# Later sums of the decays, later transposes of the context's convolved tiles

## The chip, the cores and the metric

The kernel runs on one core of a Trainium2 chip. Times are device microseconds (us) of that core. TensorE multiplies matrices, VectorE (DVE in the profile), ScalarE (ACT) and GpSimd (POOL) work on tiles in SBUF and PSUM, SyncE (SP) issues most of the DMAs. PE is TensorE, PEld its weight loads. Lower is better.

## The reference

One layer of a hybrid diffusion backbone on 512 latent tokens and a prefix of 256 context tokens, model width 1024, float32:

```
hc  = modulate(rmsnorm(ctx), csh1, csc1)          # 256 context tokens
pc  = hc @ w_in[:, :XBCDT_COLS]                   # x, B, C and dt columns
xbc_c = silu(dwconv_centred(pc[..., :CONV_CH], conv_w, conv_b))   # 5 taps along the tokens
init_states = final SSD state of the context, forward and backward
hx  = modulate(rmsnorm(x), sh1, sc1)              # 512 latent tokens
p   = hx @ w_in                                   # x, B, C, dt, gate z, pooling columns
y_x = SSD scan of both directions over 4 chunks of 128 tokens, started from init_states
x   = x + g1 * (concat(rmsnorm(y_x * silu(z)), pooling(p)) @ w_out)
x   = x + g2 * moe(modulate(rmsnorm(x), sh2, sc2))     # top 4 of 32 experts, d_ff 1024
out = rmsnorm(x)
```

The scan has 24 heads in four groups of six. The decays are `log_a = -exp(a_log) * softplus(dt)`; the scan uses their running sums within a chunk and the exponentials of these. The final state of the context is a sum over its tokens of B times (x times a weight `wdec` made from these sums).

## The kernel before, in words

The work goes in stages: modulation (to about 40 us), norms and transposes (to about 60), the context stage (to about 275), the scan of the four head groups (to about 560), the output projection and the router, and the experts (from about 600 to the end).

Products in float32 are done in three passes: `split_weights` makes a rounded part `hi` of a weight tile (L228, ScalarE) and the remainder `lo` (L231, VectorE, or every second one GpSimd for the scan's projections), and three matmuls follow: L353, L354 and L355 in `token_major`, L336, L337 and L338 in the scan's `project`. A 512-wide matmul is one of these. Weight tiles come by SyncE's DMAs into a ring `raw` of 6; `hi` and `lo` have rings of 3.

The context stage is a loop over the four groups g (L557). In each turn:

- `z_block` (turns 0, 1 and 3): the gate columns of the latent tokens, four accumulators, then tanh (L369, ScalarE) and L370 (VectorE).
- `ctx_conv(g)`: the context's projected columns (tile `ctxp`, tokens by channels) are convolved in two halves of two 128-channel blocks. A half is: four transposes to channels by tokens into a PSUM bank (L447), a copy into `xp` (L452, ScalarE), one first tap for each block (L456) and four further ones (L459) on VectorE into `ac`, tanh (L462, ScalarE), the product (L389, VectorE), four transposes back (L467) and a copy into `xc` (L468, ScalarE). `xp` and `ac` have two buffers each, `xc` two.
- `ctx_proj(g + 1)`: the next group's projection, two accumulators, copied to `ctxp`.
- `mod_row(g)`: one 1024-wide row of the modulation of the second sub-layer. Eight 512 KB blocks of w_mod come by SyncE (L417) into `mraw`, a ring of three that the bias takes part in. Even blocks go over ScalarE (L419) and a sum on GpSimd (L421), odd ones are summed on VectorE (L423, L425); L426 (GpSimd) adds both, and L432 sums over the partitions on TensorE, followed by L434 (VectorE).
- `ctx_state(g)`: `chunk_state` scales `xc` by `wdec` (L407, GpSimd) and multiplies (L409, TensorE); L477 (ScalarE) keeps the state.

Ahead of the loop stand the first `ctx_proj(0)`, the columns of dt with their softplus, and the sums of the decays (L521 to L552), which make `wdec`, `ecs` and `etot`.

The written order is not what runs. The framework's scheduler takes the instructions of the whole program, estimates times for them, and picks for each engine the order in which they stand in its queue; written order is one input of it. So projections of the scan's first group (L336 to L338, with taps L374 and L378) already run among the context's work. What each engine then does in a row is fixed when the kernel is built; at run time an engine takes its queue in that order and waits at an instruction whose inputs are not there.

Of the kernel before, what the change touches and what calls it, by code (L numbers as in the profile page):

```python
# [5 lines left out]
F32 = mybir.dt.float32  # L6
# [4 lines left out]
AF = mybir.ActivationFunctionType  # L11
ALU = mybir.AluOpType
# [4 lines left out]
P = 128  # L17
# [80 lines left out]
def mixer_and_moe(tc, a):  # L98
    nc = tc.nc
    SC, VE, PO, PE, SP = nc.scalar, nc.vector, nc.gpsimd, nc.tensor, nc.sync  # L100

    def c_(name):
        lo, hi = CONST[name]
        i = sum(lo >= c for c in CUTS[1:])
        return cons[i][:, lo - CUTS[i]:hi - CUTS[i]]
# [12 lines left out]
    pk = tc.alloc_tile_pool(name="pk", bufs=1, side="left", reuse_waits="tile")  # L118
# [13 lines left out]
    cs_scr = dram.tile([2, NT, 32, P], F32, name="cs_scr")  # L132
# [13 lines left out]
    ident = c_("ident")  # L146
# [89 lines left out]
    for k in range(KT):  # L236
        for h in range(2):
# [26 lines left out]
    def ctx_cols(g):  # L264
        return (g * GW, GW), (COL_B + g * P, P)
# [44 lines left out]
    for lo, n, which, oh_, ol_ in ((NT, NTC, 1, hch, hcl), (0, NT, 0, hxh, hxl)):  # L310
        for k in range(KT):
            tp = bank("S")
            w = n * P
            for j in range(n):
# [6 lines left out]
                                                     op=ALU.subtract)  # L321
# [3 lines left out]
    pa = tc.alloc_tile_pool(name="pctx", bufs=1, side="left", reuse_waits="tile")  # L325
# [32 lines left out]
    def ctx_proj(g):  # L358
        cps = token_major(ctx_cols(g), hch, hcl, [bank("A") for _ in range(NTC)])
        ctxp = pa.tile([P, NTC, T], F32, name="ctxp", tag="ctxp", bufs=2)  # L360
        for c in range(NTC):
            SC.activation(ctxp[:, c, :], cps[c], AF.Copy)
        return ctxp
# [48 lines left out]
    def mod_row(q):  # L412
        acc = pa.tile([P, D], F32, name="macc", bufs=1)
        acd = pa.tile([P, D], F32, name="macd", bufs=1)
        for k in range(KT):
            r = pa.tile([P, D], F32, name="mraw", bufs=3)
            SP.dma_start(r, wm[:, k, (2 + q) * D:(3 + q) * D])  # L417
            if k % 2 == 0:
                SC.activation(acc if k == 0 else r, r, AF.Copy, scale=sil[:, k, 0:1])  # L419
                if k:  # L420
                    PO.tensor_tensor(acc, acc, r, op=ALU.add)  # L421
            elif k == 1:
                VE.tensor_scalar(acd, r, sil[:, k, 0:1], None, op0=ALU.mult)  # L423
            else:
                VE.scalar_tensor_tensor(acd, r, sil[:, k, 0:1], acd, op0=ALU.mult, op1=ALU.add)  # L425
        PO.tensor_tensor(acc, acc, acd, op=ALU.add)  # L426
        mr = pa.tile([P, D], F32, name="mraw", bufs=3)[0:1, :]
        br = pa.tile([P, D], F32, name="mraw", bufs=3)[0:1, :]
        SP.dma_start(br, a["b_mod"][:, (2 + q) * D:(3 + q) * D])
        for h in range(2):  # L430
            mp = bank("S")
            PE.matmul(mp, lhsT=c_("ones"), rhs=acc[:, h * T:(h + 1) * T], start=True, stop=True)  # L432
            hs = slice(h * T, (h + 1) * T)
            VE.tensor_tensor(mr[:, hs], br[:, hs], mp[0:1, :], op=ALU.add)  # L434
        if q == 2:
            SP.dma_start(br, a["norm2_w"])
            VE.scalar_tensor_tensor(mr, mr, 1.0, br, op0=ALU.add, op1=ALU.mult)
        SC.dma_start(mod_scr[q:q + 1, :], mr)

    def ctx_conv(g, ctxp):  # L440
        xc = pa.tile([P, NTC, T], F32, name="xc", bufs=2)
        for j2 in range(2):
            tp = bank("S")
            for i in range(2):
                j = 2 * j2 + i
                for c in range(NTC):
                    PE.transpose(tp[:, i * TC + c * P:i * TC + (c + 1) * P], ctxp[:, c, j * P:(j + 1) * P], ident)  # L447
            xp = pa.tile([P, 2, TC + 4], F32, name="xp2", bufs=2)
            ac = pa.tile([P, 2, TC], F32, name="ac2", bufs=2)
            PO.memset(xp[:, :, 0:2], 0.0)  # L450
            PO.memset(xp[:, :, TC + 2:], 0.0)
            SC.activation(xp[:, :, 2:2 + TC], tp.rearrange("p (i t) -> p i t", i=2), AF.Copy)  # L452
            for i in range(2):
                j = 2 * j2 + i
                ct = g * 3 + j if j < 3 else 12 + g
                VE.tensor_scalar(ac[:, i, :], xp[:, i, 0:TC], cw[:, 0, ct:ct + 1], cb[:, ct:ct + 1],  # L456
                                 op0=ALU.mult, op1=ALU.add)
                for q in range(1, 5):
                    VE.scalar_tensor_tensor(ac[:, i, :], xp[:, i, q:q + TC], cw[:, q, ct:ct + 1], ac[:, i, :],  # L459
                                            op0=ALU.mult, op1=ALU.add)  # L460
            tt = xp[:, :, 0:TC]
            SC.activation(tt, ac, AF.Tanh)  # L462
            silu_to(ac, ac, tt)
            tp = bank("S")
            for i in range(2):
                for c in range(NTC):
                    PE.transpose(tp[:, c * TC + i * P:c * TC + (i + 1) * P], ac[:, i, c * P:(c + 1) * P], ident)  # L467
            SC.activation(xc[:, :, j2 * TC:(j2 + 1) * TC], tp.rearrange("p (c t) -> p c t", c=NTC), AF.Copy)  # L468
        return xc

    def ctx_state(g, xc):
        pair = []
# [8 lines left out]
    NA = NT + NTC  # L481
    sh3 = [P, NA, 2 * H]
    ctxps = {0: ctx_proj(0)}
# [15 lines left out]
    dt = pk.tile(sh3, F32, name="dt")  # L499
    la = pk.tile(sh3, F32, name="la")  # L500
# [16 lines left out]
    nb = pk.tile([P, NT, 2 * H], F32, name="nb")  # L517
# [3 lines left out]
    SC.activation(nega, alg, AF.Exp)  # L521
    VE.scalar_tensor_tensor(la, dt, -1.0, nega.unsqueeze(1).broadcast_to(sh3), op0=ALU.mult, op1=ALU.mult)

    F, B = slice(0, H), slice(H, 2 * H)
    wdec = pk.tile(sh3, F32, name="wdec")
    cp = bank("S")
    cpv = cp[:, 0:NA * 2 * H].rearrange("p (c h) -> p c h", c=NA)
    PE.matmul(cpv[:, :, F], lhsT=c_("slow"), rhs=la[:, :, F], start=True, stop=False, skip_group_check=True)
    PE.matmul(cpv[:, NT, F], lhsT=c_("ones"), rhs=la[:, NT + 1, F], start=False, stop=True, skip_group_check=True)
    PE.matmul(cpv[:, :, B], lhsT=c_("sup"), rhs=la[:, :, B], start=False, stop=False, skip_group_check=True)  # L530
    PE.matmul(cpv[:, NT + 1, B], lhsT=c_("ones"), rhs=la[:, NT, B], start=False, stop=True, skip_group_check=True)
    SC.activation(wdec, cpv, AF.Exp)
    VE.tensor_tensor(wdec, wdec, dt, op=ALU.mult)
    for d, (hs, tri) in enumerate(((slice(0, 32), c_("up")), (slice(16, 48), c_("lowr")))):
        cp = bank("S")
        for c in range(NT):
            PE.matmul(cp[32 * c:32 * (c + 1), 0:P], lhsT=la[:, c, hs], rhs=tri, start=True, stop=True)
        csT = pa.tile([P, P], F32, name="csT", bufs=1)
        VE.tensor_copy(csT, cp[:, 0:P])
        SC.dma_start(cs_scr[d].rearrange("c h l -> (c h) l"), csT)  # L540
    ecs = pk.tile([P, NT, 2 * H], F32, name="ecs")
    etot = pk.tile([P, NT, 2 * H], F32, name="etot")
    cp = bank("S")
    cpv = cp[:, 0:NT * 2 * H].rearrange("p (c h) -> p c h", c=NT)
    PE.matmul(cpv[:, :, F], lhsT=c_("up"), rhs=la[:, 0:NT, F], start=True, stop=True, skip_group_check=True)
    PE.matmul(cpv[:, :, B], lhsT=c_("lowr"), rhs=la[:, 0:NT, B], start=False, stop=True, skip_group_check=True)
    VE.tensor_tensor(nb, nb, cpv, op=ALU.subtract)
    SC.activation(ecs, cpv, AF.Exp)
    cp = bank("S")
    cpv = cp[:, 0:NT * 2 * H].rearrange("p (c h) -> p c h", c=NT)  # L550
    PE.matmul(cpv, lhsT=c_("ones"), rhs=la[:, 0:NT, :], start=True, stop=True, skip_group_check=True)
    SC.activation(etot, cpv, AF.Exp)  # L552


    init = [None] * G
    xcs = {}
    for g in range(G):  # L557
        if g in ZP:
            z_block(ZP.index(g), pa, "tz")
        xcs[g] = ctx_conv(g, ctxps.pop(g))  # L560
        if g + 1 < G:
            ctxps[g + 1] = ctx_proj(g + 1)
        mod_row(g)
        init[g] = ctx_state(g, xcs.pop(g))
    pa.release()
# [2 lines left out]
    pa = tc.alloc_tile_pool(name="pa", bufs=1, side="left", reuse_waits="tile")  # L568
# [237 lines left out]
    for pr in range(2):  # L806
        cath, catl = cat[pr]
        for k2 in range(6):
            tp = bank("S")
# [332 lines left out]
    for pr in range(2):  # L1142
        cs_ = (2 * pr, 2 * pr + 1)
        op = out_proj(pr, ks[4 * (pr == 0):], 2)
        for c in cs_:
            for h in range(2):
                hs = slice(h * T, (h + 1) * T)
# [608 lines left out]
```

## Time and profile before

| | |
|---|---|
| time, median of 3 runs | 1802.28 us (1801.63 to 1809.07) |
| profiled execution | 1804.47 us, its span 1802.7 us |
| mean granted TensorE clock | 0.964 |
| TensorE busy | 1635.2 us (91%), 7371 matmuls |
| VectorE busy | 1541.8 us (86%) |
| ScalarE busy | 1168.1 us (65%) |
| GpSimd busy | 621.0 us (34%) |
| DMA | 521.53 MB, mean 289 GB/s |

TensorE's busy time is the largest, but shares over the whole span mix stages. The stage of the change takes about 210 of the 1802.7 us, so it is read by itself: the stretches by engine, TensorE's waits within them, and the timelines of single engines. In a timeline a row stands for one instruction or for several of one kind in a row; the second number is then the time from the first one's start to the last one's end. The bracket at the end of a row is the time for which the engine was idle before it, and what ended that.

### The profile page before, as it was taken

What the parts mean: (1) busy time and instruction counts of PE and PEld (TensorE: products, weight loads), DVE (VectorE), ACT (ScalarE), POOL (GpSimd) and SP (SyncE); (2) the same over time, 40 slices, a digit from 0 to 9 for tenths busy, and PEclk for the clock granted to TensorE, in tenths of its full rate; (3) what the DMA queues carried; (4) which work ended last, traced back from release to release, by engine and by line L of the source; (5) the groups of instructions that cost most, each with busy time, mean ns of one, the idle gap of its engine ahead of it and who ended that gap; (6) DMA issues with size and microseconds to landing.
All of it is one profiled execution on the core that took longest, in us unless ns stands there. A gap on an engine that the chain in (4) does not pass through costs nothing. (4 is left out here: it accounts for less than half of the span.)

```text
span 1802.7 us, 21388 instructions
## 1 busy us (share of the span) xinstructions
PE 1635.2 (91%) x7371; PEld 1197.1 (66%) x7371; DVE 1541.8 (86%) x1491; ACT 1168.1 (65%) x1204; POOL 621.0 (34%) x288
## 2 busy tenths in 40 slices
PE   6998889998899799999999999998999998999985
PEld 2776667676677577767667667676666666666653
DVE  7767888987878989999989998966899999999994
ACT  6445336556643467787777877755778777787773
POOL 1303456779210102242540531501053363313303
PEclk8999899999999889999999999999999999999996
DMA  9646443223577779999999999985899999999953
GB/s 350 200 127 206 150 154 105 101 82 106 191 249 304 258 289 365 363 388 384 362 388 392 356 380 401 351 304 197 341 385 384 380 365 365 390 374 374 384 222 102
DMA packets 138561, 521.53 MB, mean 289 GB/s; under 512 B 14919, under 2 KB 45063, under 8 KB 106704
## 3 DMA queue, kind: packets, MB, share of 16 engines
q1 hardware_dynamic: 125446, 490.39, 71.6%
q0 software_dynamic: 6880, 16.79, 4.0%
q10 hardware_dynamic: 6122, 12.94, 2.1%
q8 instruction: 59, 0.97, 0.2%
q14 instruction: 54, 0.44, 0.1%
HBM read 508.78 MB, written 18.37 MB: 292 GB/s over the span
## 5 line engine op out<-in xcount | busy, mean ns | idle before, releaser
L1077 DVE TENSOR_TENSOR lo<-raw,hi 128x2048 fp32r<-128x2048 f32 x398 | 897.4, 2283 | 88.5 <-ACT hi L1076 85.5
L1076 ACT ACTIVATE hi<-raw 128x2048 fp32r<-128x2048 f32 x398 | 752.0, 1915 | 180.7 <-PE A L1305 106.7
L1328 POOL DMA_INDIRECT acc_scr<-y,ixi x32 | 239.9, 7498 | 531.2 <-DVE y L1326 450.8
L1305 PE MATMUL A<-lo,xh 128*128 128x512 f32 (+3 forms) x1072 | 310.9, 407 | 37.5 <-DVE lo L1077 32.8
L1305 PE MATMUL A<-hi,xh 128*128 128x512 f32 (+3 forms) x1072 | 304.4, 400 | 7.0 <-ACT hi L1076 3.8
L1305 PEld LDWEIGHTS A<-lo,xh 128*128 128x128 f32 (+3 forms) x1072 | 184.3, 181 | 126.9 <-DVE lo L1077 80.0
L1305 PEld LDWEIGHTS A<-hi,xh 128*128 128x128 f32 (+3 forms) x1072 | 192.2, 182 | 62.8 <-ACT hi L1076 5.6
L1099 POOL DMA_INDIRECT xg<-h_scr,ixi x30 | 114.7, 3823 | 269.4 <-PE S L1109 150.2
L1305 PE MATMUL S<-lo,ah 128*128 128x512 f32 (+3 forms) x512 | 165.8, 404 | 15.4 <-DVE lo L1077 15.3
L1305 PE MATMUL S<-hi,ah 128*128 128x512 f32 (+3 forms) x512 | 165.6, 403 | 3.8 <-DVE ah L1112 3.8
L1305 PE MATMUL A<-hi,xl 128*128 128x512 f32 (+3 forms) x544 | 153.8, 396 | 0.0
L1305 PEld LDWEIGHTS S<-lo,ah 128*128 128x128 f32 (+3 forms) x512 | 90.5, 183 | 49.8 <-DVE lo L1077 24.2
L1305 PEld LDWEIGHTS A<-hi,xl 128*128 128x128 f32 (+3 forms) x544 | 95.0, 175 | 31.4
L1305 PEld LDWEIGHTS S<-hi,ah 128*128 128x128 f32 (+3 forms) x512 | 92.6, 184 | 33.2 <-DVE ah L1112 4.0
L228 ACT ACTIVATE hi<-raw 128x1024 fp32r<-128x1024 f32 (+1 forms) x73 | 75.9, 1045 | 40.0 <-PE A L355 14.3
L231 DVE TENSOR_TENSOR lo<-raw,hi 128x1024 fp32r<-128x1024 f32 (+1 forms) x59 | 77.8, 1322 | 18.6 <-ACT hi L228 17.4
L1305 PE MATMUL S<-hi,al 128*128 128x512 f32 (+3 forms) x272 | 86.2, 396 | 0.0
L630 ACT ACTIVATE row<-row,nb 128x128 f32<-128x128 f32 x192 | 59.5, 389 | 37.4 <-POOL row L626 37.3
L336 PE MATMUL A<-hx,hi 128*128 128x512 f32 x160 | 65.8, 411 | 3.4 <-DVE at L378 2.1
L338 PE MATMUL A<-hx,lo 128*128 128x512 f32 x160 | 66.2, 414 | 0.0
L337 PE MATMUL A<-hx,hi 128*128 128x512 f32 x160 | 65.2, 408 | 0.0
L378 DVE SCALAR_TENSOR_TENSOR at<-A,cw,at 128x510 f32<-128x510 f32 (+1 forms) x80 | 57.8, 740 | 5.9 <-ACT at L374 5.4
(452 smaller groups left out, 2476.1 us busy)
## 6 DMA issues: line engine op xcount, KB each, us to landing
raw<-in_w_dram SPq DMA_DIRECT2D x384, 1024.0 KB
raw<-in_w_in_dram SPq DMA_DIRECT2D x36, 512.0 KB
mraw<-in_w_mod_dram SPq DMA_DIRECT2D x32, 512.0 KB
raw<-in_w_out_dram SPq DMA_DIRECT2D x14, 1024.0 KB
row<-cs_scr ACTq DMA_DIRECT2D x32, 384.0 KB
raw<-in_w_mod_dram SPq DMA_DIRECT2D x16, 512.0 KB
raw<-in_w_in_dram SPq DMA_DIRECT2D x16, 384.0 KB
xt<-in_x_dram SPq DMA_DIRECT2D x4, 512.0 KB
```

Of the source, the lines that this page charges most:

```text
L228: SC.activation(hi, r, AF.Copy)
L231: e.tensor_tensor(lo, r, hi.bitcast(F32), op=ALU.subtract)
L336: PE.matmul(lat, lhsT=hi[:, k, :], rhs=row_of(hxh, k), start=(k == 0), stop=False)
L337: PE.matmul(lat, lhsT=hi[:, k, :], rhs=row_of(hxl, k), start=False, stop=False)
L338: newest[0] = PE.matmul(lat, lhsT=lo[:, k, :], rhs=row_of(hxh, k), start=False, stop=(k == KT - 1))
L378: VE.scalar_tensor_tensor(ac[:, u:v], src[:, u + o:v + o], cw[:, j, ct:ct + 1], ac[:, u:v], op0=ALU.mult, op1=ALU.add)
L630: SC.activation(row[:, h, :], row[:, h, :], AF.Exp, bias=nb[:, c, i:i + 1])
L1076: ia = SC.activation(hi, r, AF.Copy)
L1077: i = VE.tensor_tensor(lo, r, hi.bitcast(F32), op=ALU.subtract)
L1099: PO.indirect_dma_start(out=t[0:m, :], out_offset=None, in_=h2_scr, in_offset=bass.IndirectOffsetOnAxis(ap=col[0:m, :], axis=0), bounds_ch ...
L1305: PE.matmul(bk[0:n, :], lhsT=u[:, k, 0:n], rhs=v[:, j * 512:(j + 1) * 512], start=(k == 0 and i == 0), stop=((last or m == LT and k == KT ...
L1328: PO.indirect_dma_start(out=acc_scr, out_offset=bass.IndirectOffsetOnAxis(ap=icol[0:m, :], axis=0), in_=y[0:m, :], in_offset=None, bounds_ ...
```

## The change

The sums of the decays become a function `decays()`, called in the first turn of the loop behind `z_block(0)`. `ctx_conv` no longer transposes back: it keeps the two `ac` tiles and returns a function `rest()` with the transposes back (now L473) and the copies to `xc` (L474) of both halves, which is called behind `ctx_proj(g + 1)`. The number of buffers stays.

```diff
     def ctx_conv(g, ctxp):
         xc = pa.tile([P, NTC, T], F32, name="xc", bufs=2)
+        acs = []
         for j2 in range(2):
...
             silu_to(ac, ac, tt)
-            tp = bank("S")
-            for i in range(2):
-                for c in range(NTC):
-                    PE.transpose(tp[:, c * TC + i * P:c * TC + (i + 1) * P], ac[:, i, c * P:(c + 1) * P], ident)
-            SC.activation(xc[:, :, j2 * TC:(j2 + 1) * TC], tp.rearrange("p (c t) -> p c t", c=NTC), AF.Copy)
-        return xc
+            acs.append(ac)
+
+        def rest():
+
+            for j2, ac in enumerate(acs):
+                tp = bank("S")
+                for i in range(2):
+                    for c in range(NTC):
+                        PE.transpose(tp[:, c * TC + i * P:c * TC + (i + 1) * P], ac[:, i, c * P:(c + 1) * P], ident)
+                SC.activation(xc[:, :, j2 * TC:(j2 + 1) * TC], tp.rearrange("p (c t) -> p c t", c=NTC), AF.Copy)
+            return xc
+
+        return rest
...
-    F, B = slice(0, H), slice(H, 2 * H)
-    wdec = pk.tile(sh3, F32, name="wdec")
-    cp = bank("S")
...
+    def decays():
+        F, B = slice(0, H), slice(H, 2 * H)
+        wdec = pk.tile(sh3, F32, name="wdec")
         cp = bank("S")
...
+        return wdec, ecs, etot
...
     for g in range(G):
         if g in ZP:
             z_block(ZP.index(g), pa, "tz")
-        xcs[g] = ctx_conv(g, ctxps.pop(g))
+        if g == 0:
+            wdec, ecs, etot = decays()
+        rest = ctx_conv(g, ctxps.pop(g))
         if g + 1 < G:
             ctxps[g + 1] = ctx_proj(g + 1)
+        xcs[g] = rest()
         mod_row(g)
         init[g] = ctx_state(g, xcs.pop(g))
```

The body of `decays()` is that of the lines it replaces. Three places show how the order of the queues changes. Line numbers of the changed kernel are its own: L447 became L448, L456 L457, L459 L460, L467 L473, and the decays' L528 to L546 became L537 to L555.

On TensorE, the first of the decays' sums (`la` is the logarithm of the decays, `con` holds constants) and the gate matmul ahead of them, before:

```order
L355 MATMUL A<-hi,hx_98 128x512
L528 MATMUL S<-la,con_110 128x6x24
L529 MATMUL S<-la,con_76 128x24
L530 MATMUL S<-la,con_110 128x6x24
L531 MATMUL S<-la,con_76 128x24
L537 MATMUL S<-con_76,la 32x128 x4
L537 MATMUL S<-con_110,la 32x128 x4
```

and after:

```order
L355 MATMUL A<-hi,hx_98 128x512
L537 MATMUL S<-la,con_110 128x6x24
L538 MATMUL S<-la,con_76 128x24
L539 MATMUL S<-la,con_110 128x6x24
L540 MATMUL S<-la,con_76 128x24
L546 MATMUL S<-con_76,la 32x128 x4
L546 MATMUL S<-con_110,la 32x128 x4
```

The rows are the same and stand at the same place in the queue.

On VectorE, the taps of group 2 (`ac_1391` is the first half's tile), the modulation row's sums (`macd`) between them, before:

```order
L425 SCALAR_TENSOR_TENSOR macd<-mraw,sil,macd 128x1024
L456 TENSOR_SCALAR ac_1391<-xp_1390,cw,cb 128x256 x2
L459 SCALAR_TENSOR_TENSOR ac_1391<-xp_1390,cw,ac_1391 128x256 x7
L425 SCALAR_TENSOR_TENSOR macd<-mraw,sil,macd 128x1024
L459 SCALAR_TENSOR_TENSOR ac_1391<-xp_1390,cw,ac_1391 128x256
L389 SCALAR_TENSOR_TENSOR ac_1391<-xp_1390,ac_1391 128x512
L231 TENSOR_TENSOR lo<-raw,hi 128x1024
L425 SCALAR_TENSOR_TENSOR macd<-mraw,sil,macd 128x1024
```

The same place after, from the second L425 on (`ac_1413` is the second half's tile, whose taps stood about 11 rows later before):

```order
L425 SCALAR_TENSOR_TENSOR macd<-mraw,sil,macd 128x1024
L460 SCALAR_TENSOR_TENSOR ac_1391<-xp_1390,cw,ac_1391 128x256 x2
L460 SCALAR_TENSOR_TENSOR ac_1413<-xp_1412,cw,ac_1413 128x256 x2
L460 SCALAR_TENSOR_TENSOR ac_1391<-xp_1390,cw,ac_1391 128x256
L425 SCALAR_TENSOR_TENSOR macd<-mraw,sil,macd 128x1024
L460 SCALAR_TENSOR_TENSOR ac_1391<-xp_1390,cw,ac_1391 128x256
L460 SCALAR_TENSOR_TENSOR ac_1413<-xp_1412,cw,ac_1413 128x256 x2
L231 TENSOR_TENSOR lo<-raw,hi 128x1024
L389 SCALAR_TENSOR_TENSOR ac_1391<-xp_1390,ac_1391 128x512
L389 SCALAR_TENSOR_TENSOR ac_1413<-xp_1412,ac_1413 128x512
L370 SCALAR_TENSOR_TENSOR yt_102<-tz,A 128x512
L370 SCALAR_TENSOR_TENSOR yt_103<-tz,A 128x512
```

The second half's taps moved up between those of the first, and both L389 now stand behind all of them.

On TensorE, the transposes back of group 2, with the last gate matmuls ahead of them, before:

```order
L354 MATMUL A<-lo,hx_94 128x512
L355 MATMUL A<-hi,hx_98 128x512
L467 MATMUL S<-con_76,ac_1391 128x128 x4
L447 MATMUL S<-con_76,ctxp 128x128 x4
L336 MATMUL A<-hx_91,hi 128x512
L337 MATMUL A<-hx_95,hi 128x512
```

and after:

```order
L354 MATMUL A<-lo,hx_94 128x512
L355 MATMUL A<-hi,hx_98 128x512
L473 MATMUL S<-con_76,ac_1391 128x128 x4
L473 MATMUL S<-con_76,ac_1413 128x128 x4
L432 MATMUL S<-macc,con_76 128x512 x2
L336 MATMUL A<-hx_91,hi 128x512
L337 MATMUL A<-hx_95,hi 128x512
```

The first transposes of the second half (L447) left this place for an earlier one, next to the first half's; both halves' transposes back now stand together, and the modulation row's L432 moved up behind them.

## Rows read from the trace of the kernel before

**Rows 1.** Which stretches: busy us (x instructions) by engine, PEclk, DMA share, GB/s.

```profile
300.00:400.00 100.00, 94.84 (x450) 74.13 (x449) 85.33 (x113) 58.52 (x148) 74.47 (x68) 0.98 0.28 91
...
700.00:800.00 100.00, 96.30 (x426) 72.15 (x424) 93.77 (x65) 78.88 (x58) 22.72 (x5) 1.00 0.99 382
```

**Rows 2.** TensorE's waits, 95 to 330 us: total, times, longest.

```profile
PE S L467 <- DVE ac L389: 13.0, 3, 5.8
...
PE A L354 <- DVE lo L231: 4.7, 2, 4.4
...
PE A L336 <- DVE at L378: 2.1, 1, 2.1
```

**Rows 3.** Ten-us stretches of the context stage, one and the sum.

```profile
200.00:210.00 10.00, 7.73 (x23) 6.11 (x24) 8.41 (x12) 4.99 (x9) 4.86 (x4) 0.52 0.38 112
...
sum 230.00, PE 207.62 PEld 161.49 DVE 180.47 ACT 107.73 POOL 106.09; mean PE 9.03 PEld 7.02 DVE 7.85 ACT 4.68 POOL 4.61
```

**Rows 4.** Timeline of TensorE, group 2: start, us, engine, line, op, count, idle before.

```profile
194.55 0.39 PE L354 MATMUL A<-lo,hx 128*128 128x512 f32 x1
...
194.78 0.39 PE L355 MATMUL A<-hi,hx 128*128 128x512 f32 x1
...
200.93 1.09 PE L467 MATMUL S<-con,ac 128*128 128x128 f32 x4 [5.77 <-DVE ac L389]
...
205.23 0.63 PE L338 MATMUL A<-hx,lo 128*128 128x512 f32 x1
...
205.66 0.63 PE L336 MATMUL A<-hx,hi 128*128 128x512 f32 x1
```

**Rows 5.** Timeline of VectorE, group 0, second half.

```profile
119.78 0.73 DVE L456 TENSOR_SCALAR ac<-xp,cw,cb 128x256 f32<-128x256 f32 x2 [0.85 <-ACT xp L452]
...
120.43 3.25 DVE L459 SCALAR_TENSOR_TENSOR ac<-xp,cw,ac 128x256 f32<-128x256 f32 x8
...
124.73 0.68 DVE L389 SCALAR_TENSOR_TENSOR ac<-xp,ac 128x512 f32<-128x512 f32 x1
```

**Rows 6.** Timeline of VectorE, group 2.

```profile
184.83 3.24 DVE L425 SCALAR_TENSOR_TENSOR macd<-mraw,sil,macd 128x1024 f32<-128x1024 f32 x1 [2.75 <-DMA mraw<-in_w_mod_dram]
...
187.99 4.89 DVE L456 TENSOR_SCALAR ac<-xp,cw,cb 128x256 f32<-128x256 f32 x2
...
192.81 4.94 DVE L459 SCALAR_TENSOR_TENSOR ac<-xp,cw,ac 128x256 f32<-128x256 f32 x7
...
197.67 1.27 DVE L425 SCALAR_TENSOR_TENSOR macd<-mraw,sil,macd 128x1024 f32<-128x1024 f32 x1
...
201.05 1.22 DVE L231 TENSOR_TENSOR lo<-raw,hi 128x1024 fp32r<-128x1024 f32 x1 [0.26 <-ACT hi L228]
...
202.28 1.28 DVE L425 SCALAR_TENSOR_TENSOR macd<-mraw,sil,macd 128x1024 f32<-128x1024 f32 x1
```

**Rows 7.** Timeline of GpSimd and SyncE's queue, group 2.

```profile
184.59 2.39 POOL L421 TENSOR_TENSOR macc<-macc,mraw 128x1024 f32<-128x1024 f32 x1 [3.58 <-ACT mraw L419]
...
194.50 2.57 POOL L421 TENSOR_TENSOR macc<-macc,mraw 128x1024 f32<-128x1024 f32 x1 [1.76 <-ACT mraw L419]
...
198.97 0.33 SPq L417 DMA_DIRECT2D mraw<-in_w_mod_dram  x1
```

**Rows 8.** Timeline of VectorE and TensorE, group 3.

```profile
234.18 7.79 DVE L459 SCALAR_TENSOR_TENSOR ac<-xp,cw,ac 128x256 f32<-128x256 f32 x3
...
245.27 0.74 DVE L378 SCALAR_TENSOR_TENSOR at<-A,cw,at 128x510 f32<-128x510 f32 x1
...
249.00 0.63 PE L467 MATMUL S<-con,ac 128*128 128x128 f32 x4 [3.34 <-DVE ac L389]
...
249.46 0.60 PE L447 MATMUL S<-con,ctxp 128*128 128x128 f32 x4
...
264.22 1.08 PE L467 MATMUL S<-con,ac 128*128 128x128 f32 x4 [3.92 <-DVE ac L389]
```

**Rows 9.** Timeline of TensorE, group 1.

```profile
151.99 0.80 PE L354 MATMUL A<-lo,hch 128*128 128x512 f32 x1 [4.39 <-DVE lo L231]
```

More of the change, by code (lines that the diff above doesn't have):

```diff
@@ L522, in mixer_and_moe @@
     VE.scalar_tensor_tensor(la, dt, -1.0, nega.unsqueeze(1).broadcast_to(sh3), op0=ALU.mult, op1=ALU.mult)
-    F, B = slice(0, H), slice(H, 2 * H)
-    wdec = pk.tile(sh3, F32, name="wdec")
-    cp = bank("S")
-    cpv = cp[:, 0:NA * 2 * H].rearrange("p (c h) -> p c h", c=NA)
-    PE.matmul(cpv[:, :, F], lhsT=c_("slow"), rhs=la[:, :, F], start=True, stop=False, skip_group_check=True)
-    PE.matmul(cpv[:, NT, F], lhsT=c_("ones"), rhs=la[:, NT + 1, F], start=False, stop=True, skip_group_check=True)
@@ L530, in mixer_and_moe @@
[L530 to L534, printed above, removed]
-        cp = bank("S")
[L536 to L552, printed above, removed]
+    def decays():
+        F, B = slice(0, H), slice(H, 2 * H)
+        wdec = pk.tile(sh3, F32, name="wdec")
+        cp = bank("S")
+        cpv = cp[:, 0:NA * 2 * H].rearrange("p (c h) -> p c h", c=NA)
+        PE.matmul(cpv[:, :, F], lhsT=c_("slow"), rhs=la[:, :, F], start=True, stop=False, skip_group_check=True)
+        PE.matmul(cpv[:, NT, F], lhsT=c_("ones"), rhs=la[:, NT + 1, F], start=False, stop=True, skip_group_check=True)
+        PE.matmul(cpv[:, :, B], lhsT=c_("sup"), rhs=la[:, :, B], start=False, stop=False, skip_group_check=True)
+        PE.matmul(cpv[:, NT + 1, B], lhsT=c_("ones"), rhs=la[:, NT, B], start=False, stop=True, skip_group_check=True)
+        SC.activation(wdec, cpv, AF.Exp)
+        VE.tensor_tensor(wdec, wdec, dt, op=ALU.mult)
+        for d, (hs, tri) in enumerate(((slice(0, 32), c_("up")), (slice(16, 48), c_("lowr")))):
+            cp = bank("S")
+            for c in range(NT):
+                PE.matmul(cp[32 * c:32 * (c + 1), 0:P], lhsT=la[:, c, hs], rhs=tri, start=True, stop=True)
+            csT = pa.tile([P, P], F32, name="csT", bufs=1)
+            VE.tensor_copy(csT, cp[:, 0:P])
+            SC.dma_start(cs_scr[d].rearrange("c h l -> (c h) l"), csT)
+        ecs = pk.tile([P, NT, 2 * H], F32, name="ecs")
+        etot = pk.tile([P, NT, 2 * H], F32, name="etot")
+        cp = bank("S")
+        cpv = cp[:, 0:NT * 2 * H].rearrange("p (c h) -> p c h", c=NT)
+        PE.matmul(cpv[:, :, F], lhsT=c_("up"), rhs=la[:, 0:NT, F], start=True, stop=True, skip_group_check=True)
+        PE.matmul(cpv[:, :, B], lhsT=c_("lowr"), rhs=la[:, 0:NT, B], start=False, stop=True, skip_group_check=True)
+        VE.tensor_tensor(nb, nb, cpv, op=ALU.subtract)
+        SC.activation(ecs, cpv, AF.Exp)
+        cp = bank("S")
+        cpv = cp[:, 0:NT * 2 * H].rearrange("p (c h) -> p c h", c=NT)
+        PE.matmul(cpv, lhsT=c_("ones"), rhs=la[:, 0:NT, :], start=True, stop=True, skip_group_check=True)
+        SC.activation(etot, cpv, AF.Exp)
+        return wdec, ecs, etot
```

## The prediction

> **What bounds the kernel now.** I read the slices of busy time first. Late in the run, from 700 to 800 us, TensorE is busy 96.30 of 100 us while the DMA engines are busy 0.99 of the time; at 300 to 400 us, in the scan, DMA is at 0.28 and TensorE at 94.84 [rows 1]. The change touches neither: it acts on the context stage, some 100 to 275 us after the start. A microsecond that TensorE loses there is passed on, because the scan has little slack to take it back and the experts wait for the router, which stands behind the scan. So a loss or gain in the context stage counts in full.
>
> Second, TensorE's waits from 95 to 330 us. The largest is L467, the transposes of the context's convolved tile back to tokens, which wait for VectorE's last instruction on that tile, L389: 13.0 us in three waits. L354 waits 4.7 us for a weight remainder (L231), L336 2.1 us for the scan's taps [rows 2]. From 100 to 330 us TensorE is busy 207.62 of 230 us, so 22.4 us idle; these three lines are 19.8 of them [rows 3]. After such a wait the clock is low: at 200 to 210 us the granted clock is 0.52 [rows 3], and two 512-wide matmuls start 0.43 us apart instead of 0.23 [rows 4], so 12 matmuls at that pace lose about 2.4 us.
>
> Third, why VectorE is late. Undisturbed, it needs 0.73 us for the two first taps of a half, 3.25 for the eight others and 0.68 for L389: 4.66 us [rows 5]. In group 2, where the largest wait stands, the same work is stretched: L425 3.24 us beside 1.27 later, L456 4.89 beside 0.73, seven L459 4.94 beside 7 x 0.41 = 2.85 [rows 6]. That is 1.97 + 4.16 + 2.09 = 8.2 us too much, all while GpSimd ran four tensor operations, the first from 184.59, the last from 194.50 us [rows 7]. In group 3 three L459 take 7.79 us instead of 1.22 [rows 8].
>
> **The change, part by part.** *The decays' sums* are written behind the first gate block. The order of the instructions has their nine rows on TensorE at the same places before and after, so this part removes, adds and moves nothing: 0 us. If it did move, its small matmuls would stand between 512-wide ones and cost well under 1 us.
>
> *The transposes back* come out of the convolution and are called behind the next group's projection. No instruction is added or removed. But the scheduler now puts the two halves of a group together: all eight L447 in a row in groups 1 to 3, then both halves' taps mixed on VectorE, then the transposes back, close together. This gives TensorE more matmuls between the first transposes and the ones back, and VectorE more work before it can release them. In the order I counted the 512-wide matmuls from the last L447 of a group to its first L467: group 2 has 53 for the first half before and 64 for both after; group 3 has 66 before and 90 after; group 0 has 63 and 49 before, 65 after, and had no wait.
>
> *Group 2.* VectorE must now do, before the last L389, the second half's own 4.66 us [rows 5], a third L425 of 1.28 and an L231 of 1.22 [rows 6]: 7.16 us more. TensorE runs out later by 11 x 0.23 = 2.53 [rows 4] and by four more L447, which take 0.46 (L467 to L447, as many transposes) [rows 8]: 2.99. The wait of 5.77 us [rows 4] grows by 4.2 to about 9.9. Then a queue: the third L425 needs a block of w_mod whose buffer becomes free only with the second L425, which ended at 198.94; SyncE issued the load at 198.97 and VectorE took the block at 202.28, so it landed within 3.3 us [rows 6, 7]. Now only five L459 (2.0 us) stand between those two L425, and both halves' last taps are queued behind the third: up to 1.3 us of standing. I take 1.3 (bounds 0 and 3.3). Group 2: +5.5.
>
> The Trainium skill ("SBUF — State Buffer", "🔬 SBUF: two separate sides") says that a VectorE operation with two SBUF inputs and a GpSimd operation share one port pair as a lock held for a whole instruction. By it one more GpSimd operation inside the longer chain would add all of its 2.4 us [rows 7], and the sum would be 2.4 higher; the 8.2 us above are what the trace shows of it, somewhat under the four operations' length.
>
> *Group 3.* VectorE has 4.66 more, five more L378 of the scan's taps by 0.74 [rows 8], and an L231 of 1.22: 9.6. TensorE has 24 x 0.23 + 0.46 = 6.0 more cover. The first wait of 3.34 [rows 8] becomes 6.9; the second, 3.92 [rows 8], is gone, as both halves are released at nearly one time. Net 6.9 - 7.26 = -0.3 (bounds -2.4, with the 2.1 at L336 hidden as well, and +3).
>
> *Group 1.* There the wait is 4.39 us at L354 [rows 9], for an L231 that stood behind seven L459. It now stands ahead of the taps but behind two L425, whose blocks come by DMA, and the next L231 behind four L456 and five L459. Between -4.4 (the wait goes) and +4 (the second L231 is late too) I take 0, since what it waits for is still late and the row gives it no earlier data.
>
> *Other places.* The modulation row's sum L432 now stands right behind the transposes, in group 2 some 60 matmuls earlier; its GpSimd sum is ready by then. One second-half gate load group moves behind the modulation's loads on SyncE; the rings ahead of it hold data, 0. If that cover fails it is the fourth case below.
>
> Sum: 0 + 5.5 - 0.3 + 0 = +5.2 us. The profiled execution took 1804.47 us with a span of 1802.7; the median of the three runs is 1802.28, and 1804.47 lies within their 1801.63 to 1809.07. So the profile's terms are added to the median: 1807.5.
>
> **The rivals.**
> *Waits joined (my forecast), 0.40.* 0 to +11 us: 1802 to 1813.
>
> *Paid back, no change, 0.21.* The second halves' taps are done early, so VectorE is ahead afterwards: the 2.1 at L336 goes, and group 1's 4.39 with it. For it: VectorE has 49.5 us idle in these 230 [rows 3]. Against it: the early work is the same work, and L354 depends on a load. 5.2 - 2.1 - 4.4 = -1.3: 1801.0.
>
> *Faster, 0.17.* VectorE's stretched taps depend on which GpSimd operation they meet. If the mixed taps miss these, group 2's wait is 9.9 + 1.3 - 8.2 = 3.0 (-2.8) and group 3's 6.9 - 6.6 = 0.3 (-7.0); with two low-clock stretches of 2.4 the sum is -14.6: 1787.7. It decides only where nearly all of both stretches goes. Against it: GpSimd's operations are released by the same data as before, and the chain is longer, so it meets more of them.
>
> *Slower, 0.22.* VectorE stands behind L425 with both halves' taps queued. L425 waited 2.75 us for its DMA at 184.83 [rows 6]. If each of the two L425 that now stand among mixed taps waits so long in groups 1 and 2, that is 4 x 2.75 = 11 in place of the 1.3: 5.2 - 1.3 + 11 = +14.9: 1817.2. For it: three buffers only, and a load that starts with the reader's end. Against it: the first of the pair mostly has its block. It decides when a landing exceeds the 2 us of taps between two L425 in both groups.
>
> *That it does not do what it says* is true of the first part, as said, and is in the sum with 0.
>
> **How the numbers follow.** The likeliest case gives 1807.5. A range from 1791 to 1817 takes in the first two cases, about a third of the faster one and most of the slower one, and leaves some 2 in 10 out; the likeliest case alone has 1802 to 1813. A measurement of this kernel can tell 0.5%, 9 us, from no change. Faster than that: most of the third case and a trace of the second, 0.16. Slower: most of the fourth and the upper end of the first, 0.24. Within: 0.60.
>
> **What would show it.** Right: the waits of L467 (now L473) in group 2 become one of some 10 to 11 us, in group 3 one of 6 to 8 us, with none at the second half; the decays' matmuls run at the same times; low clock after the same number of waits. Wrong: L473 without a wait of over 4 us (the faster case: look for L460 at 0.41 us each); L425 with DMA waits of 2 to 3 us among the taps (slower); a TensorE idle sum from 100 to 330 us that stays at 22 us or below; or a difference that lies behind 600 us, where I expect none.

## The result, and the profile after

The changed kernel takes 1814.92 us (median of 9 runs, 1807.14 to 1818.06); the kernel before took 1803.64 on the same chips (9 runs, 1801.63 to 1809.07). The ratio of the mean times is 1.0053, with a 95% interval of 1.0035 to 1.0072: some 9.6 us slower (the medians lie 11.3 apart), nearly twice the 5.2 that I forecast and inside the range. The two profiles differ by 11.0 us in their spans (1813.7 and 1802.7) and in the mean granted clock (0.956 and 0.964). Busy times hardly moved: TensorE 1640.5 us, VectorE 1532.4, GpSimd 622.5.

First TensorE's waits in the changed kernel, 95 to 345 us (engine, line, waited for: us in total, times, longest). They answer to [rows 2]:

```profile
PE S L473 <- DVE ac L389: 17.6, 2, 9.2
PE A L354 <- DVE lo L231: 6.5, 1, 6.5
PE S L656 <- ACT hi L228: 2.9, 1, 2.9
PE A L353 <- DVE yt L370: 2.7, 1, 2.7
PE S L432 <- POOL xp L452: 0.9, 1, 0.9
```

All such waits in this stretch come to 30.6 us, in the kernel before to 24.0. The three waits at the transposes back have become two, and these two are 17.6 us instead of 13.0. Where they stand (TensorE's timeline: start, us, engine, line; idle time before at the end of the row), to be read against [rows 4, 8, 9]:

```profile
156.88 0.79 PE L354 MATMUL A<-lo,hch 128*128 128x512 f32 x1 [6.48 <-DVE lo L231]
...
207.99 1.97 PE L473 MATMUL S<-con,ac 128*128 128x128 f32 x8 [8.44 <-DVE ac L389]
...
254.87 1.12 PE L473 MATMUL S<-con,ac 128*128 128x128 f32 x4 [9.20 <-DVE ac L389]
...
257.06 0.63 PE L336 MATMUL A<-hx,hi 128*128 128x512 f32 x1
257.49 0.63 PE L337 MATMUL A<-hx,hi 128*128 128x512 f32 x1
...
261.63 0.60 PE L473 MATMUL S<-con,ac 128*128 128x128 f32 x4
```

Group 1's wait at L354 is 6.48 us instead of 4.39; group 2's at L473 is 8.44 instead of 5.77; group 3's first is 9.20, and its second half, 18 matmuls later, waits no more (before 3.34 and 3.92). After the 9.20 the matmuls start 0.43 us apart, as in [rows 4]. The stretches show the same (as [rows 3]): in the ten us in which the wait of group 3 begins TensorE is busy 5.67, in the next ten, in which it ends, 5.13 at a granted clock of 0.53.

```profile
240.00:250.00 10.00, 5.67 (x26) 4.35 (x24) 10.00 (x11) 1.73 (x2) 4.99 (x2) 0.96 0.00 0
250.00:260.00 10.00, 5.13 (x15) 4.26 (x16) 10.00 (x17) 3.96 (x6) 0.00 (x0) 0.53 0.40 105
```

Why VectorE is late shows in its timeline of group 2:

```profile
186.64 3.23 DVE L425 SCALAR_TENSOR_TENSOR macd<-mraw,sil,macd 128x1024 f32<-128x1024 f32 x1 [2.82 <-DMA mraw<-in_w_mod_dram]
189.79 5.54 DVE L457 TENSOR_SCALAR ac<-xp,cw,cb 128x256 f32<-128x256 f32 x4
195.24 5.39 DVE L460 SCALAR_TENSOR_TENSOR ac<-xp,cw,ac 128x256 f32<-128x256 f32 x8
200.55 1.27 DVE L425 SCALAR_TENSOR_TENSOR macd<-mraw,sil,macd 128x1024 f32<-128x1024 f32 x1
201.75 2.06 DVE L460 SCALAR_TENSOR_TENSOR ac<-xp,cw,ac 128x256 f32<-128x256 f32 x5
203.73 1.28 DVE L425 SCALAR_TENSOR_TENSOR macd<-mraw,sil,macd 128x1024 f32<-128x1024 f32 x1
...
207.25 1.28 DVE L389 SCALAR_TENSOR_TENSOR ac<-xp,ac 128x512 f32<-128x512 f32 x2
```

and in GpSimd's of the same time:

```profile
186.38 2.41 POOL L421 TENSOR_TENSOR macc<-macc,mraw 128x1024 f32<-128x1024 f32 x1 [4.24 <-ACT mraw L419]
189.93 2.52 POOL L421 TENSOR_TENSOR macc<-macc,mraw 128x1024 f32<-128x1024 f32 x1 [1.14 <-DVE macd L425]
192.41 2.44 POOL L231 TENSOR_TENSOR lo<-raw,hi 128x1024 fp32r<-128x1024 f32 x1
196.21 2.55 POOL L421 TENSOR_TENSOR macc<-macc,mraw 128x1024 f32<-128x1024 f32 x1 [1.36 <-ACT mraw L419]
205.15 5.61 POOL L426 TENSOR_TENSOR macc<-macc,macd 128x1024 f32<-128x1024 f32 x1 [6.39 <-DVE macd L425]
```

Of VectorE's rows, L425 at 186.64 takes 3.23 us, four L457 take 5.54 (undisturbed 1.46), the next eight L460 5.39 (undisturbed 3.25): 1.96 + 4.08 + 2.14 = 8.2 us of standing (time by which a row is longer than its undisturbed length), beside GpSimd's four operations from 186.38 to 198.76. The kernel before had lost the same 8.2 us there, so what the joining adds in group 2 is VectorE's own work. From 200.55 to 205 GpSimd runs nothing, and every row has its own length: five L460 2.06, as in [rows 5]. Nor is there idle time before the L425 at 200.55 and 203.73: the DMA's blocks were there. SyncE issued the load of the second of them behind GpSimd's L421 that ended at 192.45, and not behind the second L425 as in [rows 7]:

```profile
192.47 0.33 SPq L417 DMA_DIRECT2D mraw<-in_w_mod_dram  x1
```

It goes both ways: GpSimd's L426 at 205.15, begun among VectorE's last taps, takes 5.61 us, its like elsewhere 2.4. It ends 2.2 us behind the last L389.

Group 3's joined chain holds five of these operations, two more than the first half's did before. VectorE beside the two:

```profile
241.52 1.27 DVE L425 SCALAR_TENSOR_TENSOR macd<-mraw,sil,macd 128x1024 f32<-128x1024 f32 x1
242.72 5.48 DVE L460 SCALAR_TENSOR_TENSOR ac<-xp,cw,ac 128x256 f32<-128x256 f32 x3
...
250.97 1.26 DVE L460 SCALAR_TENSOR_TENSOR ac<-xp,cw,ac 128x256 f32<-128x256 f32 x3
```

GpSimd beside it:

```profile
242.94 2.50 POOL L426 TENSOR_TENSOR macc<-macc,macd 128x1024 f32<-128x1024 f32 x1 [4.13 <-DVE macd L425]
245.40 2.53 POOL L231 TENSOR_TENSOR lo<-raw,hi 128x1024 fp32r<-128x1024 f32 x1
```

Three L460 at 242.72 take 5.48 us beside these two operations; three at 250.97, with GpSimd idle, take 1.26. Before, L426 and an L231 behind it ran after the first half's transposes and stood beside the second half, whose first taps (L456) took 2.81 us at 256.36. The joining brought their cost into the one wait.

### The profile page after: what moved, and what is told of

Its sections match the earlier page's. It is cut to its first block, busy times and chain, and to the rows that moved or that the text cites. A ratio compares the mean times of both kernels' runs of the same rounds, so it can differ in the third digit from the quotient of the medians.

```text
span 1813.7 us, 21402 instructions
## 1 busy us (share of the span) xinstructions
PE 1640.5 (90%) x7371; PEld 1202.0 (66%) x7371; DVE 1532.4 (84%) x1491; ACT 1168.3 (64%) x1204; POOL 622.5 (34%) x288
## 3 DMA queue, kind: packets, MB, share of 16 engines
q10 hardware_dynamic: 6122, 12.94, 2.1%
## 5 line engine op out<-in xcount | busy, mean ns | idle before, releaser
L228 ACT ACTIVATE hi<-raw 128x1024 fp32r<-128x1024 f32 (+1 forms) x73 | 76.0, 1045 | 31.6 <-PE A L355 10.2
L231 DVE TENSOR_TENSOR lo<-raw,hi 128x1024 fp32r<-128x1024 f32 (+1 forms) x59 | 74.4, 1261 | 18.3 <-ACT hi L228 17.4
L336 PE MATMUL A<-hx,hi 128*128 128x512 f32 x160 | 68.2, 426 | 0.0
L378 DVE SCALAR_TENSOR_TENSOR at<-A,cw,at 128x510 f32<-128x510 f32 (+1 forms) x80 | 58.1, 742 | 11.1 <-ACT at L374 10.7
```

The lines of the kernel that those rows point to most:

```text
L228: SC.activation(hi, r, AF.Copy)
L231: e.tensor_tensor(lo, r, hi.bitcast(F32), op=ALU.subtract)
L336: PE.matmul(lat, lhsT=hi[:, k, :], rhs=row_of(hxh, k), start=(k == 0), stop=False)
L378: VE.scalar_tensor_tensor(ac[:, u:v], src[:, u + o:v + o], cw[:, j, ct:ct + 1], ac[:, u:v], op0=ALU.mult, op1=ALU.add)
```

## The experiments

Each was compared with the kernel before on the same chip. Profiles of the same queues in the same order can lie 4 us apart at 340 us from the start (the first experiment's and that of the kernel before), so I read waits from profiles and time from the ratios.

**Which part does it?** First the decays alone, with `ctx_conv` as it was, transposes inside:

```diff
-        rest = ctx_conv(g, ctxps.pop(g))
+        xcs[g] = ctx_conv(g, ctxps.pop(g))
         if g + 1 < G:
             ctxps[g + 1] = ctx_proj(g + 1)
-        xcs[g] = rest()
```

> The first part of the change alone: the decays' sums behind the first gate block, the convolution as before. Each engine's queue holds the same instructions in the same order as before. Theory (the whole effect is the joining of the two halves): no difference, 1.000 within 0.002. Rival (the decays' place costs something through waits that the order does not show): 1.002 to 1.005, half or all of the change's effect.

Measured: 0.9993 (0.9981 to 1.0006). Then both parts, but with the transposes back written ahead of the projection:

```diff
         rest = ctx_conv(g, ctxps.pop(g))
+        xcs[g] = rest()
         if g + 1 < G:
             ctxps[g + 1] = ctx_proj(g + 1)
-        xcs[g] = rest()
```

> Both halves of a group are convolved before the first is transposed back, but the transposes are written ahead of the next group's projection, not behind it; the decays as in the changed kernel. Theory (joining the halves is all; the place behind the projection does nothing): as the changed kernel, 1.005 (1.0035 to 1.007), with waits at L473 of about 8.4 and 9.2 us. Rival (the deferral behind the projection is what costs): 1.000 to 1.002, with waits at L473 as before, three of 3 to 6 us.

Measured: 1.0036 (1.0023 to 1.0049), in the range of the changed kernel's 1.0053. Its queues hold the same instructions in the same order as the changed kernel's on all five engines. Its waits (95 to 345 us), the same two as after:

```profile
PE S L473 <- DVE ac L389: 17.6, 2, 9.2
PE A L354 <- DVE lo L231: 4.5, 1, 4.5
```

Those of the decays alone, three as before:

```profile
PE S L467 <- DVE ac L389: 11.0, 3, 5.4
PE A L354 <- DVE lo L231: 3.5, 2, 3.4
```

So the decays and the place behind the projection change nothing. What acts is that a group's first half is no longer written back before its second half is convolved. Over the two pairs of profiles the context's waits grow from 24.0 and 20.9 to 30.6 and 28.7: 7.2 us on the mean.

**Each group by itself.** Groups in JOIN, (2,) in one run and (3,) in the other, write both halves back together, the others half by half, and `rest()` stands ahead of the projection as in join_only:

```diff
+    JOIN = (2,)
...
+            if j2 == 0 and g not in JOIN:
+                back(0, ac)
...
+                if g in JOIN or j2 == 1:
+                    back(j2, ac)
```

> Only group 2 is joined; groups 0, 1 and 3 go half by half as before. Theory (each group's joined chain costs what its waits grow by): group 2's wait at the transposes back about 8 to 9 us instead of 5.77, the time 2 to 4 us longer (1.001 to 1.002), the waits of group 3 still two of 3 to 4 us. Rival (the loss comes from what is queued behind group 1, and group 2's is made up later): 1.000 within 0.001.

> Only group 3 is joined. Theory: one wait of 8 to 10 us instead of 3.34 and 3.92, the time 1 to 4 us longer (1.0005 to 1.002). Rival (in group 3 the joining is neutral, as I forecast, and the 9.2 us come from the groups ahead of it): one wait of 6 to 7 us, 1.000 within 0.001.

Measured: 1.0055 (1.004 to 1.007) and 1.0075 (1.006 to 1.0089). Both expectations of the time failed: one group costs as much as all four. The context explains little of it. Group 2's wait became 11.9 us, more than the 8 to 9 expected, and group 3's one wait is 8.3 us, as the theory had it; yet at 360 us join_group2 is 9 us ahead of the kernel before in its profile, and join_group3 6. Both lose all of it and more from 420 to 450 us, in the scan. The waits of join_group2 from 400 to 450 us, then its stretch of 400 to 500 us and that of the kernel before:

```profile
PE S L664 <- DVE row L657: 4.6, 1, 4.6
PE S L409 <- POOL xd L407: 2.9, 1, 2.9
```

```profile
400.00:500.00 100.00, 80.15 (x382) 62.47 (x382) 69.54 (x120) 52.37 (x125) 48.63 (x47) 0.86 0.35 125
```

```profile
400.00:500.00 100.00, 88.05 (x460) 69.19 (x459) 79.49 (x133) 60.26 (x140) 57.36 (x53) 0.95 0.41 147
```

TensorE is busy 80.15 and 80.85 us there in these two, 86.7 to 88.1 in the kernel before, the changed kernel and the first two experiments. The edit stands in the context, but the scheduler also put the scan's last group in another order. So these two runs do not price a group, and I take no number from them for that.

**Is GpSimd what holds VectorE up?** In the next four either the weight remainders of the scan's first group (L231) or the modulation rows' sums go to VectorE, each with the changed kernel and with the one before:

```diff
-    POOL_EVERY[0] = PEV
     start_group(0)
     for i in range(5):
         group_tile(0, i)
+    POOL_EVERY[0] = PEV
```

```diff
-            if k % 2 == 0:
-                SC.activation(acc if k == 0 else r, r, AF.Copy, scale=sil[:, k, 0:1])
-                if k:
-                    PO.tensor_tensor(acc, acc, r, op=ALU.add)
...
-        PO.tensor_tensor(acc, acc, acd, op=ALU.add)
+            if k == 0:
+                SC.activation(acc, r, AF.Copy, scale=sil[:, k, 0:1])
+            else:
+                VE.scalar_tensor_tensor(acc, r, sil[:, k, 0:1], acc, op0=ALU.mult, op1=ALU.add)
```

> The changed kernel, but the weight remainders (L231) of the scan's first group are all made on VectorE; before, every second one was GpSimd's, at 2.4 us, beside 1.2 us on VectorE. The order of the queues changes with it, so the waits at L473 are what to read. Theory (VectorE's joined chain is stretched by each GpSimd operation that runs beside it): the stretch from these operations goes and 1.2 us of own work come in their place, so group 2's wait falls from 8.4 to about 7, group 3's, with two such operations in its chain, from 9.2 to 6 or 7; the time 2 to 5 us under the changed kernel's. Rival (the stretch is not GpSimd's doing): the waits grow by VectorE's own work, by 1.2 and 2.4 us.

Measured: 1.0053 (1.0037 to 1.007), no gain. The two waits at L473 grew to 9.58 and 11.50 us, by 1.1 and 2.3, as the rival had it. But the rival's reason, that the stretch is not GpSimd's doing, is not what the trace shows. VectorE and then GpSimd in group 3 of this run:

```profile
238.84 2.61 DVE L460 SCALAR_TENSOR_TENSOR ac<-xp,cw,ac 128x256 f32<-128x256 f32 x1
...
245.33 0.47 DVE L460 SCALAR_TENSOR_TENSOR ac<-xp,cw,ac 128x256 f32<-128x256 f32 x1
```

```profile
238.18 2.98 POOL L421 TENSOR_TENSOR macc<-macc,mraw 128x1024 f32<-128x1024 f32 x1 [4.12 <-ACT mraw L419]
```

One L460 takes 2.61 us beside an L421 and 0.47 with GpSimd idle. Most of the remainders left GpSimd (one L231 of a later tile of the scan still runs there at 241.13), and its modulation sums came among the taps in their place: group 2's chain, from its first L425 on, met four. So this run did not take GpSimd away from the chain, and cannot decide between the two.

> The changed kernel, but a modulation row is summed by VectorE alone: seven operations of 1.27 us a row instead of 0.75 + 3 x 1.27, and none of GpSimd's four of 2.4 to 2.7 us. Theory (stretch by GpSimd): VectorE gets 4.3 us of own work a row and loses the stretch of two GpSimd operations in each chain, some 5 us, so the waits at L473 stay within 2 us of 8.4 and 9.2, and taps that meet no GpSimd operation run at 0.41 us each. Rival (no stretch by GpSimd): the waits grow by about 4 us each, the time by some 10 us.

Measured: 0.9997 (0.9987 to 1.0007). The change's loss is gone. The convolution's tile (ns min/median/max, first and last start in us) in this run:

```profile
L454 DVE SCALAR_TENSOR_TENSOR ac<-xp,cw,ac x64: 463/471/483, 106.7 to 240.2; 128x256 f32<-128x256 f32 x64
...
L451 DVE TENSOR_SCALAR ac<-xp,cw,cb x16: 398/402/2516, 106.1 to 222.6; 128x256 f32<-128x256 f32 x16
```

and in the changed kernel:

```profile
L460 DVE SCALAR_TENSOR_TENSOR ac<-xp,cw,ac x64: 468/476/2619, 104.9 to 251.8; 128x256 f32<-128x256 f32 x64
...
L457 DVE TENSOR_SCALAR ac<-xp,cw,cb x16: 399/405/2507, 104.3 to 230.2; 128x256 f32<-128x256 f32 x16
```

No further tap is longer than 0.483 us, though one first tap still meets one of the L231 that GpSimd kept. Group 2's wait at the transposes back (L467 in this run) is gone and group 3's is 6.6 us, both lower than the theory allowed (8.4 and 9.2, within 2 us):

```profile
PE A L336 <- DVE yt L370: 8.1, 1, 8.1
PE S L467 <- DVE ac L389: 6.6, 1, 6.6
PE A L336 <- DVE at L378: 4.5, 3, 2.5
```

Part of the time came back as waits of the scan's first projections (L336); the 8.1 us stand just ahead of group 2's transposes back. All waits from 95 to 345 us come to 23.9 us, as in the kernel before. The rival's 10 us more did not come, though all of VectorE's 4.3 us of own work a row was added. But TensorE's queue has another order here too: 78 and 94 of the 512-wide matmuls stand between the transposes of groups 2 and 3 and those back, where the changed kernel has 64 and 90. How much of the gain is GpSimd's absence and how much the longer cover, the run does not separate.

> The kernel before with the weight remainders (L231) of the scan's first group all on VectorE. Theory (stretch by GpSimd): the waits at L467, three of 13.0 us in all, fall by 1 to 4 us, the time is 0 to 5 us shorter (0.997 to 1.000). Rival: the waits grow by 1 to 2 us each, 1.001 to 1.003.

> The kernel before with the modulation rows summed by VectorE alone. Theory (stretch by GpSimd): as the own work of 4.3 us a row replaces a stretch of up to 5 us, the waits at L467 stay about 13 us or fall, 0.997 to 1.001. Rival: three waits grow by 2 to 4 us each, 1.003 to 1.006.

Measured: 1.0009 (0.9997 to 1.0021) and 1.0029 (1.0015 to 1.0042). The waits at the transposes back, 13.0 us in the kernel before and 11.0 in the decays' run with the same queues, are 10.5 and 10.7 us, so they fell by little that the profiles can tell. The first run has a new wait of 3.8 us, of L409 for GpSimd's `xd`; the interval of its time reaches into both ranges and decides nothing. The second time is outside what the theory allowed, and its interval reaches into the rival's. That run has the scan's other order: TensorE is busy 80.81 us from 400 to 500, with a 4.6 us wait for VectorE's row. So it tells of that order as well as of GpSimd.

**Both kinds of work off GpSimd.** Both edits together:

> The changed kernel with the modulation rows' sums and the weight remainders of the scan's first group on VectorE. With the rows' sums alone the change's loss was gone (0.9997), with the remainders alone it was not (1.0053). Theory (GpSimd's modulation sums are what holds up the joined chain; the remainders only trade 2.4 us of standing for 1.2 of own work): 0.997 to 1.001. Rival (VectorE's own work is the limit): 1.002 to 1.005, with group 2's wait back at 3 us or more.

Measured: 0.9974 (0.9962 to 0.9985), 1800.66 us beside 1804.33: in the theory's range and faster than both kernels. All taps have their own length, and there is no wait at the transposes back. First the tile, then the largest waits that are left:

```profile
L454 DVE SCALAR_TENSOR_TENSOR ac<-xp,cw,ac x64: 470/477/481, 106.5 to 242.8; 128x256 f32<-128x256 f32 x64
...
L451 DVE TENSOR_SCALAR ac<-xp,cw,cb x16: 405/407/409, 105.9 to 220.7; 128x256 f32<-128x256 f32 x16
```

```profile
PE A L336 <- ACT xp L457: 8.1, 1, 8.1
PE A L336 <- DVE yt L370: 4.1, 1, 4.1
```

These two stand a little ahead of the transposes back of group 3 and of group 2, so a part of the old waits has moved to another matmul. All waits from 95 to 345 us come to 17.8 us, against 30.6 in the changed kernel. Two L231 of later tiles stay on GpSimd in group 3 and meet two of the rows' sums on VectorE, which take 2.76 and 3.36 us beside 1.27. And the order changed again: 83 and 113 matmuls of cover for groups 2 and 3.

> The kernel before with both of GpSimd's kinds of work beside the taps on VectorE: the modulation rows' sums and the weight remainders of the scan's first group. Theory: no tap is longer than 0.48 us; the waits at L467 are what VectorE's own work leaves, 6 to 11 us. With the rows' sums alone on VectorE the time was 1.0029; I expect 1.000 to 1.004, since VectorE's own work grows by 4.3 us a row and 1.2 us a remainder. Rival: the loss there came from GpSimd's remainders, and it is now gone, under 1.000.

Measured: 1.0045 (1.0023 to 1.0066), above what was expected, though its interval takes that in; again the scan's other order (80.85 us busy from 400 to 500), two waits at the transposes back of 10.2 and 6.2 us, as expected, and one tap of 1.31 us, which was not. The half-by-half form gains nothing from it, the joined form does; how much of that is the scan's order these runs do not tell.

**The rows out of the way altogether.** The four rows behind the loop:

```diff
-        mod_row(g)
         init[g] = ctx_state(g, xcs.pop(g))
+    for g in range(G):
+        mod_row(g)
```

> The changed kernel with the four modulation rows written behind the loop instead of in each turn, so that few of their sums on GpSimd and VectorE stand among the taps. The order of the queues changes with it. Theory (the joined chain of VectorE is late because modulation sums on GpSimd hold it up): the taps run at their own 0.41 to 0.48 us, L473's two waits fall from 17.6 us in all to under 8, and the time is at or under that of the kernel before, unless the rows then hold up the scan. Rival (the second half's own work of 4.7 us a group is the main part): the waits stay at 12 us or more.

> The kernel before with the four modulation rows written behind the loop. Theory: the three waits at L467, 11 to 13 us in all, fall under 6 us, as GpSimd's sums no longer run beside the taps; the time is 0 to 8 us shorter than the kernel before, or the same if the rows take it back in the scan. Rival: the waits stay above 9 us.

Measured: 1.0251 (1.0237 to 1.0265) and 1.0372 (1.0358 to 1.0386). The waits at the transposes back did what the theory said, the times did not: with the changed kernel none is left at L473, with the kernel before one of 3.9 us. But TensorE now waits for the rows themselves, which share one sum tile and follow each other (the changed kernel with the rows behind the loop):

```profile
PE S L432 <- POOL macc L426: 61.7, 3, 25.0
```

61.7 us in three waits take back far more. Between the context's projections the rows had been covered, and that was worth more than the stretch that they cause.

## Why the prediction was right in direction and half the size

*What bounds.* Right: the stage of the change is the context, and TensorE's idle time from 100 to 330 us rose from 22.4 to 30.6 us. At the experts' first gather the changed kernel is 6.9 us behind the kernel before in its profile, at the last one 10.7. Join_only is 3.1 and 6.9 behind it, and 7.3 and 8.1 behind the decays' run, which has the queues of the kernel before. So most of the loss is made ahead of the experts. Of the 3.8 us between the gathers, where I expected nothing, most is not shown to be the change's: the decays' run drifts by 3.1 there too.

*The decays: 0.* Right, by the run of that part alone.

*Group 2: +5.5, measured +2.7.* The joining was right, and so was TensorE's cover (the work that it has before it must wait), which grew by 2.9 us (2.99 forecast). VectorE's chain from the first tap to the transposes back grew less than I had added, from 12.94 to 18.20 us: 5.3 in place of 7.16 and 1.3. With a start that is 0.3 us later, 5.3 + 0.3 - 2.9 gives the 2.7. The 1.3 us of waiting for a block of w_mod did not come, as the block's load no longer stood behind the second L425. Of the other 1.9, some 0.6 is the second L389, for which the first transposes do not wait (they start at 207.99, it ends at 208.53); and 0.76 is a wait of L389 for its tanh in the kernel before, which other work of VectorE now fills:

```profile
200.10 0.69 DVE L389 SCALAR_TENSOR_TENSOR ac<-xp,ac 128x512 f32<-128x512 f32 x1 [0.76 <-ACT xp L462]
```

*Group 3: -0.3, measured +1.9.* One wait of 9.20 for two of 7.26. The second wait went as forecast, and the cover grew by 5.8 us (6.0 forecast). The step that failed is VectorE's chain: I added its own work, 9.6 us, and left the stretch at the 6.6 us that the first half alone had met. The chain grew by 11.6: the own work by 7.6, the stretch by 4.0, to 10.6. With the longer chain, L426 and one more L231 came beside the taps, and the three L460 at 242.72 alone lost 4.2 us. The sentence on the port rule of the Trainium skill ("SBUF — State Buffer", "🔬 SBUF: two separate sides") named this price, 2.4 us for one more operation; I kept it out of the sum. The traces here bear the rule out for these operations: one tap of 0.47 us takes 2.61 beside one GpSimd operation, and with the sums off GpSimd no further tap is longer than 0.483. It also holds in the other direction, in L426's 5.61 us. In group 2 the one more operation, L426, cost VectorE nothing: it was the one held up.

*Group 1: 0, measured +2.1 at L354 and 2.7 at L353.* In join_only the two are 4.5 and 1.4 us, so +0.1 to +2.1 and 1.4 to 2.7. The L354 that waits is the second of the two that I named, whose L231 stands behind four first taps and five further ones; two of the rows ahead of it are stretched by GpSimd. At L353 TensorE waits for L370, which an L425 with its block still on the way had been put ahead of. I had taken 0 between two bounds far apart, and had not looked at L353. This is the largest miss in the sum.

*The 2.1 us at L336* are gone in both profiles with the joined order, as I had allowed in a bound. The modulation row's L432, which I took to be ready, waited 0.9 us, as L426 was held up.

*Sum.* +2.7 + 1.9 + 2.1 + 2.7 - 2.1 = +7.3, against a measured 9.6 (6.3 to 13.0 by the interval). That the sum came as near as 5.2 to 7.3 is in part luck: group 2 was 2.8 too high and L336 2.1, group 3 was 2.2 too low and group 1 4.8. I had put nothing for a slower clock after longer waits. From 100 to 280 us the granted clock is 0.92 beside 0.95; in the next 160 us TensorE is busier than before (151.93 us beside 149.63), so something may be made up there. How much each of the two is worth the runs do not separate. The changed kernel, then the kernel before (busy us by engine, clock, DMA share, GB/s):

```profile
100.00:280.00 180.00, 152.37 (x649) 118.91 (x648) 131.51 (x170) 74.94 (x104) 64.91 (x49) 0.92 0.51 158
280.00:440.00 160.00, 151.93 (x719) 119.22 (x718) 128.60 (x176) 95.36 (x238) 124.89 (x115) 0.97 0.31 97
```

```profile
100.00:280.00 180.00, 158.60 (x673) 123.22 (x672) 137.22 (x171) 78.62 (x111) 70.12 (x54) 0.95 0.52 162
280.00:440.00 160.00, 149.63 (x716) 116.50 (x714) 137.14 (x179) 95.24 (x240) 124.56 (x115) 0.98 0.31 101
```

*The rivals.* The median, 1814.92, lies outside the 1802 to 1813 of my likeliest case and near the 1817.2 of the slower one; by the ratio, 9.6 us on the 1802.28 that I started from, it would be 1811.9 and between the two. The number alone does not tell these cases apart, the waits do. They are joined as forecast, one in each of groups 2 and 3 and none at the second half, though neither is in the span that I gave (8.44 for 10 to 11, 9.20 for 6 to 8). Paid back: only the 2.1 at L336. Faster by missing GpSimd's operations: no, but no tap is stretched in after_both_ve, and that kernel is the fastest. Slower by DMA blocks: group 1 has some of it (VectorE stood 3.29 and 1.64 us for blocks, ahead of L370 and of L231), groups 2 and 3 none among the taps.

## What to carry to other kernels

Count what the other engines do beside a chain that you lengthen, not only the chain's own work: each GpSimd operation that comes to stand beside VectorE's work from SBUF to SBUF costs up to its length, and a longer chain has more of them ahead of its end. Where a scheduler sets the order, compare the queues of each part of an edit first: here two of its three parts left every queue as it was, and an edit of one group in the context cost TensorE 6 to 8 of 100 us in the scan. A gain that depends on an order should be timed with the whole program, since the same edit gained or lost by the order it fell into.

## What the runs showed of the hardware

In these rows GpSimd and VectorE hold each other up by whole operations where VectorE reads SBUF alone. In after_split_ve a VectorE tap of 0.47 us takes 2.61 and 2.62 beside GpSimd sums of 2.98 and 2.65, and in the changed kernel a GpSimd sum of 2.4 takes 5.61 among VectorE's last taps and products. First taps, which read one full tile instead of two, are held up as well: the longest L457 took 2.51 us, the median one 0.41. VectorE's L378, which reads PSUM, did not stand: 0.75 us at 219.45 in the kernel before, while GpSimd ran an L231 from 218.84 to 221.22. Beside such a chain a GpSimd sum of 2.4 us can be dearer than the same sum on VectorE at 1.27: with the rows' sums and the first group's remainders moved there, in the joined order, VectorE had more to do and the kernel was 0.26% faster. The order of the queues changed with it, so the runs do not show how much of that is GpSimd's.
